# A threshold search that sets two bits per step from three counts, on one Trainium2 core

## Chip, core and metric

The kernel runs on one core of a Trainium2 chip. The metric is the device time in microseconds (us) of one execution, as the median of several. The engines are named as the profile names them: PE is TensorE (PEld its weight loads), DVE is VectorE, ACT is ScalarE, POOL is GpSimd, SP is SyncE, which issues most DMAs. SBUF and PSUM are the on-chip memories; only PE's results go to PSUM first.

## What is computed

One inference step of a decoder of two layers for two groups of rows: a prompt of 512 rows and a sample group of 8 sequences with 4 new rows each, which has a cache of 2048 keys per sequence. In each layer, half of the channels go through a gated mix over chunks, the other half through sparse attention: a light indexer scores all keys, and each query attends to the best k of them only. Then come an output projection, layer norms, a feed-forward block and a gated embedding. The part that matters here is the selection for the sample group (k = 256 of 2052):

```python
def sample_sparse_attn(q, k_new, v_new, qi, wi, ki_new, ck, cv, cki, page_table):
    ...
    I = indexer_scores(qi, wi, ki_all)
    tpos = PAST_LEN + jnp.arange(T)
    causal = jnp.arange(L)[None, :] <= tpos[:, None]
    I = jnp.where(causal[None], I, -jnp.inf)
    _, idx = lax.top_k(I, TOPK_SAMPLE)
    ...
    return attend_selected(q, k_sel, v_sel, valid)
```

## The kernel before

All 544 rows stay on the chip. A product of 32-bit matrices is made from three products of split operands (a rounded part `hi` or `h`, and the rest `lo` or `l`), so most of PE's work is in triples of matmuls with 272 or 256 columns. The weights come from memory in chunks (`raw`), ACT rounds them (`hi`), DVE or POOL subtracts (`lo`).

The order of all instructions is fixed when the kernel is built. The work is written as some fifty generators (`backbone`, `s_scores`, `unit` and so on); each says before a piece of work which engine it takes and for how long, and `Sched.run` lays the pieces out one after the other by estimated start times and by a table of priorities (`PR`, weights `WP` and `WO`). At run time each engine then takes its instructions in that order, and semaphores hold it where data isn't there.

`s_scores` works once per layer. It makes the scores of the sample queries (`y.I`, 128 partitions with 513 scores each: a query's keys are spread over four partitions) and finds for each query the threshold that just 256 scores exceed, as a bit pattern of a 32-bit number from the highest bit down:

- `count(thr)` (lines 1300 to 1307) has ACT take the sign of (threshold - score) over the 513 scores and add the signs up in `cf` (line 1302; the signs themselves go to the scratch `maskb`). PE multiplies `cf`, 128 x 1 and 32 bits wide, by the constant matrix `gallf`, which adds up the four partitions of a query (the matmul's own line is that of the helper `mm`, 828).
- DVE compares the sum with a limit and makes the bit (line 1315), and sets it in `c` together with the next bit to try (line 1317).
- One count with the threshold zero (`zero`) decides on the sign (lines 1310 and 1311), then 31 steps follow, one bit each.

So 32 counts a layer go round ACT, PE and DVE. A 16-bit copy of the same matrix, `gall`, serves three products after the search. Around the search, other generators fill the engines: on DVE above all the top-k of the prompt's queries (`MAX8` and `MATCH_REPLACE8`, lines 1229 and 1231) and the rotations (`rope`, lines 1006 to 1012); on PE the backbone's products (`mm<-hi,Ah` and its kin), the rotated sample queries spread over partitions (`at<-cp,u` in `q_sample`), the transposes of gathered keys (`at<-ident,w`, line 1689 in `s_qk`) and their small products with the sample queries (`at<-w,QB` in `s_kt`); on ACT and DVE the evictions from PSUM (`copy`, lines 865 and 867) and the gated mix (lines 1490 to 1553).

Of the kernel before, what the change touches and what calls it, by code (L numbers as in the profile page):

```python
# [8 lines left out]
F32 = mybir.dt.float32  # L9
F32R = mybir.dt.float32r  # L10
BF16 = mybir.dt.bfloat16
F16 = mybir.dt.float16
# [44 lines left out]
WO = 10.415  # L57
PR = {'q_sample': 10.5, 'free_raw': 7.5, 'gmix': 2.0, 'evac_c1': 11.0, 's_scores': 17.0, 's_block': 14.0, 'mix_b': 3.5, 'load_r': 8.5, 'kidx': 14.5, 's_attn': 3.0, 'evac_au': -2.5, 'head': 1.5, 's_kt': 6.0, 'loads': 3.0, 'evac_q': -4.0, 'sgu_load': 14.0, 's_relu': 1.5, 'mix_a': 14.5, 'setup1': 6.0, 's_attn_f': 12.5, 'gmlp': 4.5, 'unit': 0.0, 'load_pe': 6.5, 'evac_oa': 1.0, 'backbone': -6.5, 'evac_c0': -1.5, 'setup2': 0.5, 'splits': -2.5, 's_qk': 6.0, 'gnorm': 1.0, 'store': 7.0, 'setup': 6.0, 'wout22': -0.5, 'wadd': 12.0, 'mtee': 4.0, 'fin': 0.5, 'wsum': 7.0, 'wcopy': 0.5, 'evac_p': 10.0, 'ln1': 5.0, 'moving': -1.0, 'vload': 15.5, 'split_x': 12.0, 'evac_f2': 16.5, 'warm': 8.0, 'wsplit': 5.0, 'mv': 5.0, 'evac_o': 9.5, 'wout': 11.5, 'ln2': 10.5, 'evac_g': 3.0}
# [354 lines left out]
def build(tc, I, O, cols):  # L413
# [15 lines left out]
    def const(name, shape, dt=F32):  # L429
        return sb.tile(list(shape), dt, tag=name, name=name)  # L430
# [18 lines left out]
    gallf = const("gallf", [128, 128])  # L449
# [89 lines left out]
    def setup2():  # L539
# [6 lines left out]
        G.tensor_copy(gallf, st[:, 0:128])  # L546
# [700 lines left out]
    def s_scores(y):  # L1247
# [43 lines left out]
        cf = sm("cf", [128, 1])  # L1291
        c = sm("c", [128, 1], I32)
        d = sm("d", [128, 1], I32)
# [3 lines left out]
        dp = ps[:, 8:9].bitcast(I32)  # L1297
        lim = NQ - 2 * STOP + 0.5

        def count(thr):  # L1300
            yield [("A", 707.0)]
            A.activation(y.maskb, Iv, AF.Sign, scale=-1.0, bias=thr, accum_out=cf)
            S.cur.ready += MARGIN
            yield [("P", 140.0)]
            mm(ps[:, 0:1], gallf, cf, True, True)
            S.cur.ready += 100.0
# [3 lines left out]
        V.tensor_scalar(d, ps[:, 0:1], lim, -float(2 ** 31), op0=ALU.is_gt, op1=ALU.mult)  # L1310
        V.tensor_scalar(c, d, 31, 2 ** 30, op0=ALU.arith_shift_right, op1=ALU.bitwise_xor)
        for bit in range(30, -1, -1):
            yield from count(c.bitcast(F32))
            yield [("V", 70.0)]
            V.tensor_scalar(dp, ps[:, 0:1], lim, float(2 ** bit), op0=ALU.is_gt, op1=ALU.mult)
# [1125 lines left out]
```

## Time and profile before

| | us |
|---|---|
| median of 3 runs | 1504.61 (1498.2 to 1511.35) |
| profiled execution | 1507.94 |
| its span, first to last instruction | 1506.1 |
| PE busy | 1452.1 (96%) |
| DVE busy | 1094.3 (73%) |
| ACT busy | 800.5 (53%) |
| POOL busy | 159.9 (11%) |

The profile is of one execution. Its durations are in us or ns; the start of a row is counted from the start of the span. Matmuls overlap in the pipeline, so the time that one costs is read from end to end (start plus duration), not from its duration. Idle time in front of an instruction is shown in brackets with what ended it.

### The profile page before, as it was taken

The page shows a single profiled execution, that of the slowest core. Times are in us where ns is not written, and L with a number is a line of the kernel's source. Part 1 is how long each engine was busy: PE and PEld are TensorE (multiplying, and loading weights), DVE is VectorE, ACT ScalarE, POOL GpSimd, SP SyncE. Part 2 cuts the span into 40 slices and gives each one's busy share as a digit, 9 for nine tenths or more (in the row PEclk, how much of TensorE's full clock was granted, in tenths as well). Part 3 has the DMA queues.
Part 4 walks back from the last instruction along what each step waited for, and adds up shares of the span by engine and source line. Part 5 has one row for each costly group of instructions (what it writes and reads, how often), then busy time and mean ns, then how long its engine had stood idle before and what let it go on. Part 6 is the DMA issues. An engine that isn't in the chain of part 4 may idle for free.

```text
span 1506.1 us, 31220 instructions
## 1 busy us (share of the span) xinstructions
PE 1452.1 (96%) x12262; PEld 1381.6 (92%) x12262; DVE 1094.3 (73%) x2867; ACT 800.5 (53%) x1865; POOL 159.9 (11%) x192
## 2 busy tenths in 40 slices
PE   9998999999999999999999889999999999999997
PEld 8787888799999999999987788788999999999996
DVE  5699886588965948567666998856979567484765
ACT  6747766464642715335376478663737345172443
POOL 2123421120000000001001234110200000000000
PEclk9999899999999999999999999999999999999998
DMA  7644431422231322315044425332122313232211
GB/s 236 201 147 125 146 128 59 142 85 71 85 127 57 126 86 74 123 58 185 34 149 146 155 90 175 112 135 82 69 85 99 126 57 113 76 107 99 82 60 60
DMA packets 55474, 164.47 MB, mean 109 GB/s; under 512 B 7648, under 2 KB 15008, under 8 KB 55328
## 3 DMA queue, kind: packets, MB, share of 16 engines
q1 hardware_dynamic: 44960, 124.73, 25.0%
q0 software_dynamic: 10368, 37.75, 7.6%
q8 instruction: 96, 1.57, 0.4%
q14 instruction: 50, 0.41, 0.1%
HBM read 156.09 MB, written 6.37 MB: 108 GB/s over the span
## 4 chain that ended last, share of the span: by engine, by line
PE 82%; DVE 11%; ACT 3%; DMA 2%; issue 2%; another core or an unknown queue 1%; SPq 0%; ACTq 0%; DVEq 0%
PE at L828 41%; PE mm L828 37%; DVE u L1231 2%; DVE m L1229 2%; PE at L1689 1%; PE at L1597 1%; DVE ga L861 1%; DMA raw<-in_w_c 1%; DVE t L1530 1%; DMA raw<-in_w_au 0%; PE at L1857 0%; DMA Bh<-in_x 0%; DMA w<-in_ck,idxK 0%; DVE u L1553 0%
## 5 line engine op out<-in xcount | busy, mean ns | idle before, releaser
L731 ACT CAST hi<-raw 128x1024 fp32r<-128x1024 f32 (+5 forms) x137 | 139.1, 1020 | 188.8 <-PE mm L828 89.9
L828 PE MATMUL mm<-Bh,hi 128*128 128x272 f32 x584 | 171.5, 294 | 1.3 <-DVE t L1010 0.8
L828 PE MATMUL mm<-Ah,hi 128*128 128x272 f32 x584 | 170.8, 293 | 0.3
L735 DVE TENSOR_TENSOR lo<-raw,hi 128x1024 fp32r<-128x1024 f32 (+5 forms) x122 | 144.5, 1184 | 34.8 <-ACT hi L731 34.0
L828 PE MATMUL mm<-Bl,hi 128*128 128x272 f32 x584 | 169.3, 290 | 0.0
L828 PE MATMUL mm<-Bh,lo 128*128 128x272 f32 x584 | 168.8, 289 | 0.0
L828 PE MATMUL mm<-Al,hi 128*128 128x272 f32 x584 | 168.7, 289 | 0.0
L828 PE MATMUL mm<-Ah,lo 128*128 128x272 f32 x584 | 168.2, 288 | 0.0
L828 PE MATMUL at<-w,hi 128*128 128x272 f32 x704 | 159.3, 289 | 0.0
L2069 DVE TENSOR_TENSOR u<-u,mm 128x272 f32<-128x272 f32 x96 | 42.0, 437 | 120.0 <-PE mm L828 119.0
L690 ACT CAST hi<-u 128x512 fp32r<-128x512 f32 x128 | 73.1, 619 | 96.9 <-PE mm L828 40.7
L828 PE MATMUL at<-w,lo 128*128 128x272 f32 x416 | 120.0, 288 | 0.0
L828 PEld LDWEIGHTS at<-w,hi 128*128 128x128 f32 x704 | 119.6, 188 | 0.0
L828 PEld LDWEIGHTS mm<-Bh,hi 128*128 128x128 f32 x584 | 110.7, 189 | 2.7 <-ACT hi L731 1.3
L690 ACT CAST hi<-raw 128x1024 fp32r<-128x1024 f32 x64 | 53.4, 834 | 112.4 <-PE at L828 43.7
L828 PEld LDWEIGHTS mm<-Ah,hi 128*128 128x128 f32 x584 | 110.0, 188 | 1.6 <-DVE u L1905 0.7
L828 PEld LDWEIGHTS mm<-Bh,lo 128*128 128x128 f32 x584 | 110.8, 190 | 0.3
L828 PEld LDWEIGHTS mm<-Bl,hi 128*128 128x128 f32 x584 | 110.5, 189 | 0.0
L828 PEld LDWEIGHTS mm<-Ah,lo 128*128 128x128 f32 x584 | 110.1, 189 | 0.2
L828 PEld LDWEIGHTS mm<-Al,hi 128*128 128x128 f32 x584 | 109.8, 188 | 0.0
L828 PE MATMUL at<-Bl,hi 128*128 128x272 f32 x376 | 108.6, 289 | 0.0
L828 PE MATMUL at<-Ah,lo 128*128 128x272 f32 x376 | 108.6, 289 | 0.0
(389 smaller groups left out, 4405.8 us busy)
## 6 DMA issues: line engine op xcount, KB each, us to landing
raw<-in_w_f SPq DMA_DIRECT2D x128, 512.0 KB
raw<-in_w_q SPq DMA_DIRECT2D x16, 512.0 KB
raw<-in_w_o SPq DMA_DIRECT2D x16, 512.0 KB
raw<-in_w_g SPq DMA_DIRECT2D x16, 512.0 KB
raw<-in_w_au SPq DMA_DIRECT2D x8, 512.0 KB
raw<-in_w_av SPq DMA_DIRECT2D x8, 512.0 KB
u<-in_x SPq DMA_DIRECT2D x8, 272.0 KB
hD<-t SPq DMA_DIRECT2D x16, 136.0 KB
```

What stands on the lines that cost most here:

```text
L690: A.copy(hi[:, :n], x)
L731: A.copy(c.hi[:, a:b], c.raw[:, a:b])
L735: E.tensor_tensor(c.lo[:, a:b], c.raw[:, a:b], c.hi[:, a:b].bitcast(F32), op=ALU.subtract)
L828: PE.matmul(out, l, r, start=start, stop=stop, skip_group_check=True)
L861: f(*args, **kw)
L1229: V.max(m8, work[:, :N])
L1231: V.match_replace(work[:, :N], m8, work[:, :N], -3.3e38)
L1530: E.tensor_tensor(av[:n, :256], av[:n, :256], y.sb[:n, hs], op=ALU.add)
L1597: PE.transpose(p[:, c * 128:(c + 1) * 128], P[:, c * 128:(c + 1) * 128], ident)
L1689: PE.transpose(p[:, t, :], raw[:, (g * 4 + t) * 128:(g * 4 + t + 1) * 128], ident)
L2069: V.tensor_tensor(r[:, a:b], r[:, a:b], ps[:, :n], op=ALU.add)
```

## The change

A step now sets two bits. Three thresholds are tried at once (the two bits as 01, 10 and 11), ACT makes three sign passes into three columns of `cf`, and one product counts for all three; the number of counts above the limit (0 to 3) is the pair of bits. `cf` is half precision now, which holds sums of 513 signs exactly, and the matrix is `gall`; `gallf` is gone. 15 steps set 30 bits, a count before them decides on the sign and one behind them on the last bit. DVE has three operations behind each count (compare and add up; scale to a bit pattern; set it in three thresholds) and a fourth that prepares the next step's pattern (`pre`) while ACT counts. The patterns come from a table (`tab`), which DVE writes into the counts' PSUM tile before the first count. The table of priorities and its weight `WO` have changed, too (13 entries of `PR`).

```diff
-WO = 10.415
+WO = 10.199
...
-        G.tensor_copy(gallf, st[:, 0:128])
...
-        cf = sm("cf", [128, 1])
-        c = sm("c", [128, 1], I32)
-        d = sm("d", [128, 1], I32)
+        cf = sm("cf", [128, 3], F16)
+        c = sm("c", [128, 3], I32)
...
         ps = yield Al("at", [128, 512])
-        dp = ps[:, 8:9].bitcast(I32)
+        di = ps[:, 8:9].bitcast(I32)
+        pre = sm("pre", [128, 3], I32)
+        tab = ps[:, 16:64].bitcast(I32).rearrange("p (k j) -> p k j", j=3)
+        yield [("V", 70.0 * 19)]
+        for j in range(3):
+            V.memset(tab[:, 0, j:j + 1], (j + 1) * 2 ** 29)
+        for i in range(1, 15):
+            V.tensor_scalar(tab[:, i, :], tab[:, i - 1, :], 0.25, None, op0=ALU.mult)
+        V.memset(tab[:, 15, :], 1)
+        V.tensor_copy(pre, tab[:, 0, :])
         lim = NQ - 2 * STOP + 0.5
 
-        def count(thr):
-            yield [("A", 707.0)]
-            A.activation(y.maskb, Iv, AF.Sign, scale=-1.0, bias=thr, accum_out=cf)
+        def count(*thr):
+            for j, t in enumerate(thr):
+                yield [("A", 707.0)]
+                with nc.allow_low_precision(reason="sums of 513 signs are exact"):
+                    A.activation(y.maskb, Iv, AF.Sign, scale=-1.0, bias=t, accum_out=cf[:, j:j + 1])
             S.cur.ready += MARGIN
             yield [("P", 140.0)]
-            mm(ps[:, 0:1], gallf, cf, True, True)
+            mm(ps[:, :len(thr)], gall, cf[:, :len(thr)], True, True)
             S.cur.ready += 100.0
 
         yield from count(zero)
         yield [("V", 270.0)]
-        V.tensor_scalar(d, ps[:, 0:1], lim, -float(2 ** 31), op0=ALU.is_gt, op1=ALU.mult)
-        V.tensor_scalar(c, d, 31, 2 ** 30, op0=ALU.arith_shift_right, op1=ALU.bitwise_xor)
-        for bit in range(30, -1, -1):
-            yield from count(c.bitcast(F32))
+        V.tensor_scalar(di, ps[:, 0:1], lim, -float(2 ** 31), op0=ALU.is_gt, op1=ALU.mult)
+        V.scalar_tensor_tensor(c, di.to_broadcast([128, 3]), 31, pre, op0=ALU.arith_shift_right, op1=ALU.bitwise_xor)
+        for i in range(15):
+            k = 29 - 2 * i
             yield [("V", 70.0)]
-            V.tensor_scalar(dp, ps[:, 0:1], lim, float(2 ** bit), op0=ALU.is_gt, op1=ALU.mult)
+            V.scalar_tensor_tensor(pre, tab[:, i + 1, :], 2 << k, c[:, 0:1].to_broadcast([128, 3]), op0=ALU.bitwise_xor, op1=ALU.bitwise_xor)
+            yield from count(*(c[:, j:j + 1].bitcast(F32) for j in range(3)))
             yield [("V", 70.0)]
-            V.scalar_tensor_tensor(c, dp, (2 ** (bit - 1)) if bit else 0, c, op0=ALU.bitwise_xor, op1=ALU.bitwise_xor)
+            V.tensor_scalar(ps[:, 4:7], ps[:, 0:3], lim, None, op0=ALU.is_gt, op1=ALU.add, accum_out=c2)
+            yield [("V", 70.0)]
+            V.tensor_scalar(di, c2, float(2 ** k), None, op0=ALU.mult)
+            yield [("V", 70.0)]
+            V.tensor_tensor(c, di.to_broadcast([128, 3]), pre, op=ALU.bitwise_xor)
+        c = c[:, 0:1]
+        yield from count(c.bitcast(F32))
+        yield [("V", 140.0)]
+        V.tensor_scalar(di, ps[:, 0:1], lim, None, op0=ALU.is_gt)
+        V.tensor_tensor(c, di, c, op=ALU.bitwise_xor)
         thr = c.bitcast(F32)
```

How the instructions stand now, at three places. Lines below 1285 are two lower in the changed kernel than in the one before, and a number behind a name only tells buffers apart.

DVE at the start of the first layer's search, before: `u_838` are the scores, `u_1478` and `u_1480` the rotation of the sample queries, `u_982` and `u_761` the prompt's top-k.

```order
L1287 TENSOR_SCALAR u_838<-at_847 128x512
L861 TENSOR_TENSOR ga_1438<-gs_935 128x4
L1231 MATCH_REPLACE u_982<-m_1273,u_982 128x256
L861 SCALAR_TENSOR_TENSOR gq_937<-gq_937,ga_1438 128x4
L1231 MATCH_REPLACE u_761<-m_1173,u_761 128x512
L1006 TENSOR_TENSOR u_1478<-at_574,cp 128x512
L861 TENSOR_SCALAR gq_937<-gq_937 128x4
L1009 TENSOR_TENSOR u_1480<-at_574,cp 128x8x32
L1010 TENSOR_TENSOR u_1480<-at_574,cp 128x8x32
L861 TENSOR_SCALAR gy_1439<-gq_937 128x4
L1012 TENSOR_TENSOR u_1478<-u_1478,u_1480 128x512
L1310 TENSOR_SCALAR d<-at_1461 128x1
```

And in the changed kernel, where `u_1451` and `u_1453` are the rotation and `at_1460` the tile of the counts with the table:

```order
L1285 TENSOR_SCALAR u_836<-at_845 128x512
L1004 TENSOR_TENSOR u_1451<-at_572,cp 128x512
L1299 MEMSET at_1460 128x1 x3
L1301 TENSOR_SCALAR at_1460<-at_1460 128x3 x14
L1302 MEMSET at_1460 128x3
L1303 COPY pre<-at_1460 128x3
L1007 TENSOR_TENSOR u_1453<-at_572,cp 128x8x32
L1008 TENSOR_TENSOR u_1453<-at_572,cp 128x8x32
L859 TENSOR_TENSOR ga_1436<-gs_933 128x4
L1010 TENSOR_TENSOR u_1451<-u_1451,u_1453 128x512
L859 SCALAR_TENSOR_TENSOR gq_935<-gq_935,ga_1436 128x4
L1229 MATCH_REPLACE u_980<-m_1271,u_980 128x256
```

The table's 19 operations stand inside the rotation, and the replacements of the top-k, which stood ahead of the rotation, stand behind it.

PE between two counts in the first half of the first layer's search, before (`at_1461` are the counts):

```order
L828 MATMUL at_1461<-cf,gallf 128x1
L1689 MATMUL at_2070<-ident,w_1639 128x128 x4
L1689 MATMUL at_2081<-ident,w_1639 128x128 x4
L828 MATMUL at_2090<-w_1919,QB 32x128 x4
L828 MATMUL at_2091<-w_1919,QB 32x128 x4
L828 MATMUL at_2090<-w_2069,QB 32x128 x4
L828 MATMUL at_2091<-w_2069,QB 32x128 x4
L828 MATMUL at_1461<-cf,gallf 128x1
```

And in the changed kernel, between the seventh and the eighth count of three (`at_1460`):

```order
L826 MATMUL at_1460<-cf,gall 128x3
L826 MATMUL at_1940<-w_1947,QB 32x128 x4
L826 MATMUL at_1941<-w_1947,QB 32x128 x4
L1707 MATMUL at_1998<-ident,w_1705 128x128 x4
L1707 MATMUL at_2024<-ident,w_1705 128x128 x4
L826 MATMUL at_1940<-w_1997,QB 32x128 x4
L826 MATMUL at_1941<-w_1997,QB 32x128 x4
L1707 MATMUL at_2039<-ident,w_1927 128x128 x4
L1707 MATMUL at_2060<-ident,w_1927 128x128 x4
L826 LDWEIGHTS gall
L826 MATMUL at_1460<-cf,gall 128x3
```

Two groups of small products stand between the counts in both, with eight transposes before and sixteen now.

ACT around one count early in the first layer's search, before (`t_` are tiles of the gated mix):

```order
L867 COPY w_1547<-at_1548 128x512
L1302 ACTIVATE maskb,cf<-u_838,c 128x513
L1490 ACTIVATE t_1560,gs_941<-at_1576 32x128
L1525 ACTIVATE t_1378<-t_1378,gn_1440,gy_1439 128x128
L1490 ACTIVATE t_1560,gs_941<-at_1576 32x128
```

And in the changed kernel, the second step's three passes:

```order
L729 CAST hi_1464<-raw_1452 128x1024
L1310 ACTIVATE maskb,cf<-u_836,c 128x513
L865 COPY w_1567<-at_1599 128x512
L1310 ACTIVATE maskb,cf<-u_836,c 128x513
L1508 ACTIVATE t_1563,gs_939<-at_1577 32x128
L1310 ACTIVATE maskb,cf<-u_836,c 128x513
```

Three passes stand where one stood, with a copy and an activation of other work between them.

## Rows read from the trace of the kernel before

**Rows 1.** From the page: busy time of each engine, and the chain by engine.

```profile
PE 1452.1 (96%) x12262; PEld 1381.6 (92%) x12262; DVE 1094.3 (73%) x2867; ACT 800.5 (53%) x1865; POOL 159.9 (11%) x192
...
PE 82%; DVE 11%; ACT 3%; DMA 2%; issue 2%; another core or an unknown queue 1%; SPq 0%; ACTq 0%; DVEq 0%
```

**Rows 2.** Stretches: length; busy us of PE, PEld, DVE, ACT, POOL; clock, DMA share, GB/s.

```profile
100.00:212.00 112.00, 100.19 (x946) 90.10 (x939) 102.19 (x366) 80.26 (x222) 38.52 (x42) 0.92 0.41 131
849.00:958.00 109.00, 96.65 (x940) 86.73 (x933) 98.61 (x364) 81.97 (x228) 41.28 (x44) 0.95 0.44 144
```

**Rows 3.** Timeline of PE around one count: start us, duration us, engine and operation.

```profile
139.34 0.28 PE L828 MATMUL mm<-lo,Ah 128*128 128x256 f32 x1
139.45 0.28 PE L828 MATMUL at<-cf,gallf 128*128 128x1 f32 x2
139.59 0.36 PE L828 MATMUL mm<-hi,Ah 128*128 128x256 f32 x1
139.79 0.27 PE L828 MATMUL mm<-hi,Al 128*128 128x256 f32 x1
```

**Rows 4.** Timeline of PE around a half-precision count behind the search.

```profile
211.64 0.29 PE L828 MATMUL mm<-Al,hi 128*128 128x272 f32 x1
211.77 0.18 PE L828 MATMUL at<-cnt,gall 128*128 128x1 f16 x1
211.81 0.37 PE L828 MATMUL mm<-Ah,hi 128*128 128x272 f32 x1
```

**Rows 5.** Waits of PE by releaser: us in total, times, longest us.

```profile
PE at L828 <- ACT maskb L1302: 6.7, 7, 1.8
...
PE at L828 <- DVE d L1310: 1.6, 1, 1.6
```

**Rows 6.** Timeline of all engines in one quick step of the second search.

```profile
881.02 0.28 PE L828 MATMUL at<-cf,gallf 128*128 128x1 f32 x2
...
881.33 0.17 DVE L1315 TENSOR_SCALAR at<-at 128x1 int32<-128x1 f32 x1
...
881.60 0.16 DVE L1317 SCALAR_TENSOR_TENSOR c<-at,c 128x1 int32<-128x1 int32 x1
...
881.86 0.73 ACT L1302 ACTIVATE maskb<-u,c 128x513 bf16<-128x513 f32 x1
...
882.49 0.19 ACT L1302 ACTIVATION_READ_ACCUMULATOR maskb<-u,c 128x1 f32 x1
```

**Rows 7.** Timeline of PE in the first search: small products and transposes.

```profile
134.29 1.08 PE L828 MATMUL at<-w,QB 128*32 128x128 f32 x32
135.30 1.09 PE L1689 MATMUL at<-ident,w 128*128 128x128 f32 x8
136.15 0.36 PE L828 MATMUL mm<-hi,Ah 128*128 128x256 f32 x1
```

**Rows 8.** Timeline of DVE at the start of the first search.

```profile
101.37 0.68 DVE L1287 TENSOR_SCALAR u<-at 128x512 f32<-128x512 f32 x1
...
103.16 0.68 DVE L1006 TENSOR_TENSOR u<-at,cp 128x512 f32<-128x512 f32 x1
...
105.22 0.15 DVE L1310 TENSOR_SCALAR d<-at 128x1 int32<-128x1 f32 x1
105.41 0.15 DVE L1311 TENSOR_SCALAR c<-d 128x1 int32<-128x1 int32 x1
105.48 0.15 DVE L861 TENSOR_TENSOR ga<-gy 128x4 f32<-128x4 f32 x1
```

**Rows 9.** As rows 2: the pieces of the searches in which the PE clock was lowered.

```profile
100.00:115.00 15.00, 13.05 (x109) 8.85 (x102) 14.84 (x57) 7.77 (x27) 3.31 (x2) 0.77 0.58 200
...
145.00:160.00 15.00, 11.88 (x99) 10.06 (x98) 12.62 (x49) 9.53 (x23) 4.08 (x6) 0.68 0.38 118
...
849.00:865.00 16.00, 12.25 (x99) 8.68 (x92) 15.08 (x58) 9.85 (x31) 3.30 (x2) 0.79 0.57 198
...
895.00:910.00 15.00, 13.65 (x135) 12.60 (x134) 13.69 (x54) 9.44 (x26) 7.21 (x12) 0.89 0.09 25
```

More of the change, by code (lines that the diff above doesn't have):

```diff
@@ L56 @@
 WP = 0.698
-WO = 10.415
-PR = {'q_sample': 10.5, 'free_raw': 7.5, 'gmix': 2.0, 'evac_c1': 11.0, 's_scores': 17.0, 's_block': 14.0, 'mix_b': 3.5, 'load_r': 8.5, 'kidx': 14.5, 's_attn': 3.0, 'evac_au': -2.5, 'head': 1.5, 's_kt': 6.0, 'loads': 3.0, 'evac_q': -4.0, 'sgu_load': 14.0, 's_relu': 1.5, 'mix_a': 14.5, 'setup1': 6.0, 's_attn_f': 12.5, 'gmlp': 4.5, 'unit': 0.0, 'load_pe': 6.5, 'evac_oa': 1.0, 'backbone': -6.5, 'evac_c0': -1.5, 'setup2': 0.5, 'splits': -2.5, 's_qk': 6.0, 'gnorm': 1.0, 'store': 7.0, 'setup': 6.0, 'wout22': -0.5, 'wadd': 12.0, 'mtee': 4.0, 'fin': 0.5, 'wsum': 7.0, 'wcopy': 0.5, 'evac_p': 10.0, 'ln1': 5.0, 'moving': -1.0, 'vload': 15.5, 'split_x': 12.0, 'evac_f2': 16.5, 'warm': 8.0, 'wsplit': 5.0, 'mv': 5.0, 'evac_o': 9.5, 'wout': 11.5, 'ln2': 10.5, 'evac_g': 3.0}
+WO = 10.199
+PR = {'q_sample': 10.5, 'free_raw': 7.5, 'gmix': 2.5, 'evac_c1': 11.0, 's_scores': 17.0, 's_block': 10.0, 'mix_b': 3.5, 'load_r': 9.5, 'kidx': 12.5, 's_attn': -1.5, 'evac_au': -3.5, 'head': 1.5, 's_kt': 6.0, 'loads': 3.0, 'evac_q': -4.0, 'sgu_load': 15.0, 's_relu': 1.5, 'mix_a': 14.5, 'setup1': 6.0, 's_attn_f': 12.5, 'gmlp': 4.5, 'unit': -1.0, 'load_pe': 6.5, 'evac_oa': 1.0, 'backbone': -6.5, 'evac_c0': -1.5, 'setup2': 0.5, 'splits': -2.5, 's_qk': 6.0, 'gnorm': 1.0, 'store': 7.0, 'setup': 6.0, 'wout22': -0.5, 'wadd': 12.0, 'mtee': 4.0, 'fin': -1.0, 'wsum': -0.5, 'wcopy': 9.0, 'evac_p': 10.0, 'ln1': 5.0, 'moving': -1.0, 'vload': 15.5, 'split_x': 8.0, 'evac_f2': 16.5, 'warm': 5.5, 'wsplit': 5.0, 'mv': 5.0, 'evac_o': 9.5, 'wout': 11.5, 'ln2': 10.5, 'evac_g': 3.0}
 TBS = (3, 1, 2, 0)
@@ L448, in build @@
     gall = const("gall", [128, 128], F16)
-    gallf = const("gallf", [128, 128])
     gneg = const("gneg", [128, 128], F16)
```

## Prediction

> **What bounds the kernel now.** I read the page's busy times and chain first: TensorE (PE) is busy for 96% of the span, and the chain that ended last runs on PE for 82% [rows 1]. So a microsecond comes off the end only if it comes off PE's stream. The next view is the table of stretches. The threshold search of the sample group runs once per layer, in the stretches from 100 to 212 us and from 849 to 958 us; in these 112 and 109 us PE is busy for 100.2 and 96.7 us only and VectorE (DVE) is busy for 102.2 and 98.6, ScalarE (ACT) for 80.3 and 82.0 [rows 2]. What is lost there is 24 us of waiting, plus what a lower clock costs. The search is a serial loop, ACT counts signs, PE sums over partitions, DVE sets a bit, and PE takes its instructions in a fixed order, so a count that isn't ready stops everything behind it. The changed order differs from the old one on PE only inside these two stretches and the 35 to 45 us behind each (two runs of some 930 and 950 rows of 10,215); before, between and after them it is the same row for row.
>
> **The counts on PE.** Now each of the 64 counts (32 a layer) is a product with 32-bit operands and takes two passes, x2 in its row [rows 3]. In a dense place the product before the count ends at 139.34 + 0.28 = 139.62 us and the one behind it at 139.59 + 0.36 = 139.95, where the next follows after 0.11 to 0.12: the count costs 0.33 - 0.12 = 0.21 us [rows 3]. The trace has a count with half-precision operands too, made after the search: 211.64 + 0.29 = 211.93 to 211.81 + 0.37 = 212.18, which is 0.25 - 0.12 = 0.13 us [rows 4]. Its width of one column should hold for three. Afterwards there are 17 counts a layer: 64 x 0.21 = 13.4 us become 34 x 0.13 = 4.4 us, **-9.0 us**, all on the path. The bounds are 0.06 (the count hidden under the load for the next) and 0.21, that is -11.4 and -6.3.
>
> **The waits for counts.** PE waits 6.7 us in 7 places for the sign pass [rows 5]. These places go with their steps, **-6.7 us**, and new ones come. How long is a step when nothing is in its way? In one of the quickest the count starts at 881.02, DVE's two operations at 881.33 and 881.60, the sign pass at 881.86, and its sum is read by 882.49 + 0.19 = 882.68 [rows 6]; with 0.2 for the way back to PE, an estimate (DVE started 0.03 after the count's end), that is 1.9 us. The new step has two more sign passes at 0.82 each (0.63 to the sum's read and 0.19 for it; all three write the same scratch, so each waits for the one before), one more DVE operation at 0.27 and a second sum to read: 1.9 + 1.64 + 0.27 + 0.2 = 4.0 us. What does the order give PE to do meanwhile? 32 records of small products (two groups) take 135.30 - 134.29 = 1.0 us and eight transposes 136.15 - 135.30 = 0.9 [rows 7]. At the place shown in the order, early in the search, PE has two groups of small products and sixteen transposes between two counts, 1.0 + 1.8 = 2.8 us against 4.0: 1.2 us of waiting. The second step has the same and one product of 256 columns, 0.4 more: 0.8 of waiting. The others hold 4 to 6 us by the same costing, about 4.7 on the mean, and I put no wait on them. For two layers: 2 x (1.2 + 0.8) = **+4.0 us**. The bounds are 0 (PE behind its plan anyhow) and 0.5 for each of 30 steps, 15 us.
>
> The Trainium skill ("ScalarE: Activation LUTs", section "What ACT_TABLE_LOAD costs") has an activation with a pointer for its bias at about 280 ns + 0.833 ns an element, and back-to-back ones overlapping by 93 ns: by the page three passes over 513 would be an estimated 1.94 us. The rows have 0.82 for one with the read of its sum, which the page doesn't count, so the rows' 2.5 us stands; by the page the new waits would be some 2.4 us smaller.
>
> **The table.** Before the loop DVE now builds a table of 3 x 16 words in PSUM, 19 small operations in one block, each waiting for the one before. Two dependent ones start 105.22 and 105.41, 0.19 apart; an independent one follows at 105.48, 0.07 later [rows 8]. So the block takes 17 x 0.19 + 2 x 0.07 = 3.4 us, with bounds of 1.3 and 3.6. The order puts it into the rotation of the sample queries, behind that rotation's first product, while two replacements of the prompt's top-k that stood ahead go behind it. These filled 102.05 (101.37 + 0.68) to 103.16, 1.1 us [rows 8]. So the rotation, done shortly before 105.3 now, ends 3.4 - 1.1 = 2.2 to 2.3 us later; I take 2.2. PE has nothing else in its order there: it stands idle for 1.6 us at this very place, set down to DVE's operation of line 1310 [rows 5]. That grows to 3.8: 2 x 2.2 = **+4.4 us**, with bounds of 0 and 2 x 3.6. Next the first count of three: on DVE the two replacements and two operations, until about 109.0, then three sign passes, count ready at about 111.7; PE's work behind the rotation (2.0 us at full clock, twice that at half) is through at 109.5 to 111.5. I take the middle, 1.3 us, so **+2.6 us** for two layers.
>
> **The rest.** The 15 extra counts a layer put 30 x 0.82 = 25 us onto ACT, which has 30 us free in each stretch [rows 2]. The copy of the 32-bit matrix on GpSimd goes, early and long before use: nothing. The new priorities move some rotations from GpSimd to DVE, evictions between ACT and DVE, and on SP one weight load by five places: nothing on the mean, but they are why the range is wide: -8 to +8, as large as the waits for DVE and evictions in these stretches. The later feed-forward stretches have the same PE order and hardly a wait.
>
> **Sum.** -9.0 - 6.7 + 4.0 + 4.4 + 2.6 = -4.7 us. The profiled execution took 1507.94, so 1503.2 on its footing; the median of the runs is 1504.61, 3.3 lower and inside 1498.2 to 1511.35. I forecast 1504.6 - 4.7 = 1500 us, with 1491 to 1508 for this case by itself.
>
> **Rivals.** First, the clock stays up. The granted clock was 0.77, 0.68, 0.79 and 0.89 in four pieces of the search [rows 9]; from full speed and half speed (2.4 and 1.2 GHz) that is 6.9 + 9.6 + 6.7 + 3.3 = 26.5 us at half, costing 13 us. The pieces lie where PE waits, for counts among others. If half as many steps leave fewer holes, up to 13 us come on top: 1487, or 1493 if only the two later pieces go. Against it: the start, where two of the pieces lie, gets more idle, not less. The Trainium skill ("TensorE: Matmul & The Clock Gate", "What's actually happening") says that the low clock is the resting state which activity lifts; by that rule the longer wait for the table keeps the start at half speed, and the trace agrees that the start is low (0.77).
>
> Second, DVE is the bound of the stretch. It is over 90% busy [rows 2], and it gets the table (3.4) and, for 64 operations of 0.16, some 64 again with 15 reads of sums, put at half an operation: 3.4 + 15 x 0.08 = 4.6 us more a layer. Where PE only follows DVE, its saving becomes waiting: 1504.6 + 9.2 = 1514. Against it: few of PE's waits are DVE's, and the prompt's top-k, most of DVE's load, is work whose place can move.
>
> Third, the three passes on ACT take over: slower. The order now puts other work between the three passes of a step (a copy, an activation at the place shown). At a sign pass's 0.82 each, two such make the step 5.6 us, and with DVE's queue ahead of its four operations 6.0. Against 4.7 us of PE work that is 1.3 x 30 = 39 us of waits, less 9.0 and 6.7, so 1504.6 + 23 = 1528. It decides from a mean step of 5.2 us. Against it: these orders were laid out with such work in the count.
>
> **How the numbers follow.** Forecast 0.46, clock 0.30, DVE 0.16, ACT 0.08. A median of this kernel tells about 1% from no change, 1489.6 and 1519.7. Faster: most of the clock's case and the lower edge of mine, 0.28. Slower: nearly all of ACT's case and the upper edge of DVE's, 0.08. Same: 0.64. The range of 1484 to 1515 holds the first three cases nearly whole.
>
> **What would show it.** Right: 34 count records in half precision, each 0.13 us between its neighbours; PE waiting near 4 us for the rotation at both starts; about 1 us of waiting at the count behind the sixteen transposes; steps of 4.5 to 6 us and a search some 10 to 15 us shorter. Wrong: a table much shorter than 3 us, waits for the sign pass above 15 us in all, or a granted clock of 1.00 in the pieces named. A time under 1489 would mean that the waits and the clock, not the counts, were what the search cost.

## The result, and the profile after

The changed kernel takes 1521.82 us in the median of 4 runs (1518.59 to 1522.28), against 1505.4 for the kernel before beside it: a ratio of 1.0117, with an interval of 1.0087 to 1.0147. It is slower, by 1.2% where 0.3% faster was forecast. Two later groups of runs, on other occasions, gave 1.0144 (1.0100 to 1.0188) and 1.0053 (1.0032 to 1.0075). The changed kernel's median was 1522 to 1526 in all three; that of the kernel before was 1502 to 1505 twice and 1512 to 1515 in the other groups, at much the same granted clocks (0.974 to 0.982 in the one kind, 0.971 to 0.982 in the other). So the sign holds, and the size lies between 0.5 and 1.4%. Why the level of the kernel before moves by 10 us from one group to the next was not found; groups 2 and 3 of the table below, one of either kind, ran on the same chip.

The page of the changed kernel, in answer to [rows 1]: busy times and the chain by engine.

```profile
PE 1454.3 (96%) x12168; PEld 1381.6 (91%) x12168; DVE 1115.6 (73%) x2961; ACT 813.3 (53%) x1898; POOL 147.5 (10%) x176
...
PE 76%; DVE 16%; ACT 3%; DMA 3%; issue 2%; SPq 0%; POOL 0%; ACTq 0%; DVEq 0%
```

DVE is busy for 21 us more, and its share of the chain went from 11 to 16%, while PE's fell by 6 points. Next the stretches of [rows 2], and the whole stage from the eviction of the scores to the first tanh behind the attention, layer by layer (columns: stretch, its length, busy us of PE, PEld, DVE, ACT, POOL, clock). First the changed kernel:

```profile
100.00:212.00 112.00, 93.23 (x913) 81.54 (x912) 107.17 (x409) 87.60 (x250) 34.81 (x35) 0.92 0.44 145
849.00:958.00 109.00, 91.38 (x891) 79.60 (x890) 103.54 (x394) 87.52 (x255) 36.78 (x40) 0.92 0.46 144
...
103.12:346.87 243.75, 219.82 (x2075) 197.81 (x2068) 198.92 (x707) 159.80 (x422) 54.30 (x50) 0.92 0.34 115
855.44:1097.48 242.04, 217.95 (x2071) 195.66 (x2064) 197.16 (x698) 161.03 (x426) 52.97 (x54) 0.94 0.35 116
```

The same two stages in the kernel before:

```profile
102.05:339.44 237.39, 219.66 (x2122) 198.24 (x2115) 189.80 (x660) 151.24 (x395) 63.23 (x61) 0.96 0.36 118
848.97:1082.72 233.75, 217.00 (x2130) 195.81 (x2123) 186.68 (x657) 154.38 (x402) 57.58 (x58) 0.97 0.36 120
```

This table holds the result. The stages are 6.4 and 8.3 us longer, 14.7 us together, and the span grew by 14.5; the rest of the program is as long as before. PE's free time in them (length less busy) goes from 17.7 and 16.8 to 23.9 and 24.1 us, **13.5 us more**. PE's busy time is the same to 1.1 us, though its counts should take 9 us less: the clock is 0.92 and 0.94 in place of 0.96 and 0.97, which I read as slower matmuls using up what the counts gave. DVE is busy 9.1 and 10.5 us longer. In the first search, 100 to 212 us, it is now busy for 107.2 of 112 us, 96%.

The searches themselves did come out shorter: from the first count to the last 96.6 and 89.8 us, where the kernel before has 106.6 and 103.1. The stages are longer all the same, for other work of PE moved behind the searches (in the first layer it is busy for 136.9 us there, 123.9 before). Of PE's 13.5 us of new waiting 10.1 lie in front of the last counts, and the clock fell most behind the last counts, from there to the end of the stage: from 0.99 to 0.92 in the first layer (209.6 to 339.4 us before, 203.9 to 346.9 now) and from 0.99 to 0.95 in the second.

The counts themselves cost what was forecast. The timeline of PE around a count of three:

```profile
160.28 0.28 PE L826 MATMUL mm<-lo,Ah 128*128 128x256 f32 x1
160.40 0.18 PE L826 MATMUL at<-cf,gall 128*128 128x3 f16 x1
160.44 0.37 PE L826 MATMUL mm<-hi,Ah 128*128 128x256 f32 x1
```

From 160.56 to 160.81 are 0.25 us, less 0.12 for the product behind: 0.13, as with one column in [rows 4]. The waits of PE, in answer to [rows 5] (us in total, times, longest):

```profile
PE at L826 <- DVE gy L859: 7.6, 2, 4.6
PE at L826 <- ACT maskb L1310: 6.2, 4, 2.2
PE at L826 <- DVE pre L1303: 4.8, 2, 2.4
PE at L826 <- DVE t L1357: 4.2, 2, 3.6
...
PE at L826 <- DVE gq L859: 2.6, 2, 1.3
```

The wait for the sign pass is where it was (6.2 us for 6.7); four waits for DVE, 19.2 us in all, are new or longer: three for small operations, and `t`, the 513-wide comparison behind the search. One is the table. DVE's and PE's timelines at the start of the first search (in brackets PE's idle time in front):

```profile
103.73 0.33 DVE L1299 MEMSET at<- 128x1 int32 x3
104.09 2.82 DVE L1301 TENSOR_SCALAR at<-at 128x3 int32<-128x3 int32 x14
106.99 0.06 DVE L1302 MEMSET at<- 128x3 int32 x1
107.09 0.16 DVE L1303 COPY pre<-at 128x3 int32<-128x3 int32 x1
...
107.30 0.16 PE L826 MATMUL at<-cf,gall 128*128 128x1 f16 x1 [2.40 <-DVE pre L1303]
```

The table takes 3.5 us (107.25 less 103.73). PE waits 2.4 us for it and 1.3 for the rotation (`gq`) behind it. Another wait is a stall beside POOL, the longest of PE's row for `gy`:

```profile
147.70 2.98 DVE L859 SCALAR_TENSOR_TENSOR gy<-ga,gy 128x4 f32<-128x4 f32 x1
148.29 2.36 POOL L733 TENSOR_TENSOR lo<-raw,hi 128x1024 fp32r<-128x1024 f32 x1
...
152.16 0.66 PE L826 MATMUL at<-w,QB 128*32 128x128 f32 x8 [4.59 <-DVE gy L859]
```

An operation of four columns, 0.15 us elsewhere, ends as POOL's subtraction ends (150.68 and 150.65), and PE stands still for 4.6 us, the stall and what DVE still had to do behind it. The Trainium skill ("SBUF — State Buffer", section "SBUF: two separate sides") has a DVE operation with two SBUF inputs and a GpSimd operation that reads SBUF lock each other out: the one that starts first has the port for its whole length. These rows agree in that the two end together. They do not bear out the order: DVE's row starts 0.59 us before POOL's, and DVE is the one held up. The kernel before has such stalls, too, the longest of 3.02 us at 865.7.

### The profile page after: what moved, and what is told of

It is laid out like the page before. It is cut to its first block, busy times and chain, and to the rows that moved or that the text cites. A ratio compares the mean times of both kernels' runs of the same rounds, so it can differ in the third digit from the quotient of the medians.

```text
span 1520.6 us, 31091 instructions
## 1 busy us (share of the span) xinstructions
PE 1454.3 (96%) x12168; PEld 1381.6 (91%) x12168; DVE 1115.6 (73%) x2961; ACT 813.3 (53%) x1898; POOL 147.5 (10%) x176
## 4 chain that ended last, share of the span: by engine, by line
PE 76%; DVE 16%; ACT 3%; DMA 3%; issue 2%; SPq 0%; POOL 0%; ACTq 0%; DVEq 0%
PE at L826 38%; PE mm L826 35%; DVE u L1229 3%; DVE m L1227 3%; DMA w<-in_cv,idxV 1%; PE at L1615 1%; DVE lo L733 1%; DVE ga L859 1%; ACT maskb L1310 1%; DVE w L863 1%; DMA raw<-in_w_c 1%; DMA Bh<-in_x 0%; PE at L1875 0%; DVE u L1601 0%; PE at L1707 0%
## 5 line engine op out<-in xcount | busy, mean ns | idle before, releaser
L733 DVE TENSOR_TENSOR lo<-raw,hi 128x1024 fp32r<-128x1024 f32 (+3 forms) x123 | 147.1, 1196 | 39.6 <-ACT hi L729 39.5
L826 PE MATMUL mm<-Ah,hi 128*128 128x272 f32 x584 | 174.5, 299 | 0.6 <-DVE u L1913 0.3
L826 PE MATMUL at<-Al,hi 128*128 128x272 f32 x376 | 108.9, 290 | 0.0
```

The lines of the kernel that those rows point to most:

```text
L733: E.tensor_tensor(c.lo[:, a:b], c.raw[:, a:b], c.hi[:, a:b].bitcast(F32), op=ALU.subtract)
L826: PE.matmul(out, l, r, start=start, stop=stop, skip_group_check=True)
```

## The experiments

Eighteen runs were made, in five groups, each group on one chip beside the kernel before. Ratios are to that kernel in the same group, with their 95% intervals. The expectations speak of theories. A: the steps of the new search are too long for the order. B: the new order places the work badly. C: DVE's small operations stall beside POOL's subtractions. D: what the change puts on DVE costs. E: the extra sign passes on ACT cost.

| group | before, us | run | us | ratio |
|---|---|---|---|---|
| 1 | 1512.5 | f16_onebit | 1511.3 | 0.9980 (0.9962 to 0.9999) |
| 1 | | table_ready | 1522.5 | 1.0063 (1.0042 to 1.0084) |
| 1 | | one_pass | 1520.7 | 1.0054 (1.0035 to 1.0072) |
| 1 | | new_search_old_numbers | 1527.1 | 1.0085 (1.0065 to 1.0106) |
| 2 | 1502.5 | after_again | 1526.2 | 1.0144 (1.0100 to 1.0188) |
| 2 | | table_ready_one_pass | 1517.2 | 1.0098 (1.0074 to 1.0123) |
| 2 | | subtract_on_dve | 1517.5 | 1.0096 (1.0061 to 1.0130) |
| 2 | | table_ready_replanned | 1525.5 | 1.0138 (1.0095 to 1.0181) |
| 3 | 1515.0 | two_bits_old_order | 1522.5 | 1.0057 (1.0040 to 1.0075) |
| 3 | | two_bits_old_order_table | 1525.2 | 1.0060 (1.0043 to 1.0077) |
| 3 | | after_less_topk | 1512.4 | 0.9989 (0.9974 to 1.0003) |
| 3 | | before_less_topk | 1498.6 | 0.9891 (0.9873 to 0.9909) |
| 4 | 1514.5 | after_third | 1521.7 | 1.0053 (1.0032 to 1.0075) |
| 4 | | before_more_dve | 1525.0 | 1.0082 (1.0056 to 1.0108) |
| 4 | | after_copies_on_act | 1525.3 | 1.0074 (1.0050 to 1.0098) |
| 4 | | f16_copies_on_act | 1512.0 | 0.9991 (0.9971 to 1.0010) |
| 5 | 1513.8 | two_bits_old_order_two_passes | 1525.1 | 1.0073 (1.0054 to 1.0091) |
| 5 | | f16_more_act | 1516.0 | 1.0020 (1.0006 to 1.0035) |

### One part of the change, or one part undone

**f16_onebit** does one part alone, in the kernel before:

```diff
-        cf = sm("cf", [128, 1])
+        cf = sm("cf", [128, 1], F16)
...
-            mm(ps[:, 0:1], gallf, cf, True, True)
+            mm(ps[:, 0:1], gall, cf, True, True)
```

> The kernel before with one thing changed: the sums of the signs and the matrix that adds them are half precision, so each of the 64 counts is one pass on PE and not two. The order on PE, DVE and ACT is that of before. By the rows of before a count goes from 0.21 to 0.13 us: 64 x 0.08 = 5 us less work on PE. If PE's work bounds the search (the reasoning of the prediction), the time falls by those 5 us, to 1500. If the search is bound by the chain of the steps and what feeds PE, the saving turns into waiting and the time stays at 1504 to 1506. The granted clock shows no change by either.

Measured: 0.998, some 3 us by the ratio for the 5 us taken from PE (0.2 to 5.7 by its interval; the medians lie 1.2 us apart). It is the lowest ratio of a kernel that does all the work.

**table_ready** makes the table in the program's setup, on POOL; **one_pass** makes one sign pass a step and leaves two out, so that it no longer finds the threshold; **table_ready_one_pass** does both.

```diff
+        for j in range(3):
+            G.memset(tab[:, 0, j:j + 1], (j + 1) * 2 ** 29)
+        for i in range(1, 15):
+            G.tensor_scalar(tab[:, i, :], tab[:, i - 1, :], 0.25, None, op0=ALU.mult)
...
-        for j in range(3):
-            V.memset(tab[:, 0, j:j + 1], (j + 1) * 2 ** 29)
...
+                  if j == 0:
```

> The changed kernel with the table of 3 x 16 words made once at the program's start by GpSimd, in SBUF, so that 18 of the 19 operations at the start of each search are gone from DVE; the order on PE and ACT is the same row for row. Theory A (the steps of the new search are too long for the order: table, three passes, four operations): PE's 3.7 us of waiting at the start of each search fall to 1 or less and the steps behind start 2 to 3 us earlier, 4 to 7 us in all: 1515 to 1518. Theory B (the new numbers place the work badly, the search itself is not what costs): the 3 us show up again at the next wait, 1520 to 1522. Theory C (DVE's small operations stall beside GpSimd's subtractions): the time changes by less than 3 us either way, by which operation happens to meet a subtraction.

> The changed kernel with one sign pass a step in place of three; the other two counts of a step are sums of zeros, so the search is left out in its meaning and its bits are not those of the reference, while all of its products and DVE's operations stay; the order on PE and DVE is the same row for row, but for one memset a layer. It takes 2 x 0.82 us from each of 30 steps, 49 us of ACT's work on the chain of the search. Theory A (steps too long): the waits of PE in the search go from 18 and 15 us to about 10 each, as before the change, and the clock returns: 1506 to 1512. Theory B (numbers) and theory C (stalls beside GpSimd): ACT was no bound, the time stays above 1517.

> The changed kernel with both cuts: the table made at the program's start, and one sign pass a step in place of three (the bits of the search are not the reference's). The order on PE is the same. Apart the two cuts took 0.5 and 0.6% off the ratio of 1.012. Theory A (the steps and the table are too long for the order): both add up, 1.001 or less, that is 16 us under the changed kernel, and with 9 us less of PE's work the ratio can go to 0.995. Theory C (what is left is DVE stalled beside GpSimd, or the order's own): 1.003 to 1.007, no more than either cut alone.

Measured: 1.0063 and 1.0054, no less than the 1.0053 that the changed kernel itself has beside a kernel before of the same level (after_third). Both cuts together gave 9 us on the changed kernel of their own group (1.0098 for 1.0144), with intervals that overlap, and still stand 1% above the kernel before. So the table and the passes are a part of the loss at most, and theory A falls as the main cause: one_pass takes 41 us off ACT (771.9 for 813.3 us busy on the pages) and gains nothing clear. For the table the answer is clouded by a price of its own: its 18 small operations on POOL delayed the first gather of the indexer's keys, and PE waited for that before the search began. The wait is in all five profiles with the table on POOL and in none with it on DVE; table_ready, waits of PE in the first 110 us:

```profile
PE at L1063 <- DMA w<-in_cki,idxI: 2.8, 1, 2.8
```

**after_again** and **after_third** are the changed kernel as it is:

> The changed kernel once more as it is, for its profile and its ratio on the chip of the three runs beside it. Every theory: a ratio of 1.009 to 1.015 to the kernel before, and per layer 24 us of waiting of PE between the scores and the first tanh.

> The changed kernel as it is, beside the three others on one chip. Every theory: 1.009 to 1.016 to the kernel before.

The second missed its range: 1.0053, with 1521.7 us as ever, beside a kernel before at 1514.5.

**subtract_on_dve** takes POOL's 1024-wide subtractions during the searches to DVE:

```diff
+                if S.search and b - a == 1024:
+                    E = V
```

> The changed kernel with the 1024-wide subtractions of the weights' low parts that GpSimd makes during the searches (7 in all, 2.36 us each) made by DVE, in the same place of the order; PE, ACT and SP have the same rows. It takes away what DVE's small operations stall beside (stalls of 2 to 2.8 us, 7 of them in the searches) and gives DVE 7 times some 1.1 us of its own work. Theory C (the stalls are what costs): PE's waits for gy and t, 7.6 and 4.2 us, fall to under 3 in all and the ratio comes to 1.003 to 1.007. Theory A: DVE has only more to do in a search that its steps bound; the ratio stays at 1.010 to 1.016.

Measured: 1.0096, 8.7 us under the changed kernel of its group, again with intervals that overlap. PE's waits for `gy` and `t` went from 7.3 + 4.3 to 2.7 + 3.7 us, but it now waits 9.6 us in 7 places for the subtractions on DVE. The stalls beside POOL are a part of the loss at most.

### The order

**new_search_old_numbers** has the search of the change with `WO` and `PR` of before; **table_ready_replanned** plans anew for a ready table, with the rotations' small operations kept off POOL's subtractions in the plan.

> The changed kernel's search with the scheduler's numbers (weight and priorities) of the kernel before. Theory B (the new numbers place the work badly): the time comes to the prediction's sum or below, 1495 to 1503. Theory A (steps too long for any order whose costs are the planner's): 1515 to 1530, with PE waiting over 15 us in each search. Theory C: the stalls beside GpSimd fall elsewhere, 1510 to 1525.

> The changed kernel with the table made at the program's start and the planner told so (70 ns in place of 1330 for the start), and with the small operations of the rotations marked for the planner as ones that do not run beside a GpSimd subtraction. The order is planned anew from there. Theory A and C together: each search starts 3.5 us earlier and PE does not wait for gy beside a subtraction, ratio 0.995 to 1.003. Theory B (it is the placing that costs, and any new plan throws dice): anywhere from 0.995 to 1.015, with waits at new places.

Measured: 1.0085 and 1.0138. Other orders of the new search are no better, and the first lies where theory A had it (1515 to 1530), not B (1495 to 1503). The strongest test of the order is **two_bits_old_order**, where the new step fills the slots of two old ones and PE's order is that of before, 30 counts fewer:

```diff
+            yield from slots(lambda: (sign(0, t[0]), sign(1, t[1])), lambda: None)
...
+            yield from slots(lambda: sign(2, t[2]), lambda: total(3))
```

> The new search laid into the order of the kernel before: planner's costs, numbers and slots are those of before, and a step of two bits fills the slots of two old steps (two sign passes in the first, the third and the product in the second), with the table made at the program's start by GpSimd. PE's order is that of before but for 30 counts fewer; so the search is as long as before and its steps have twice the time. Theory B (the new order packs the search too tightly: the form itself costs little): the counts' 9 us are gained and some of the 6.7 of waits: ratio 0.990 to 0.997, 1490 to 1500. Theory D (DVE's extra operations a step cost wherever they lie) or A (the three passes cost wherever they lie): ratio 1.003 to 1.012.

> As the run beside it (the new search in the order of before), but with the table made by DVE in PSUM at the start of each search, as in the changed kernel; no time is planned for it. Every theory: PE waits some 2 to 4 us more at the start of each search, 4 to 8 us in all on the run beside it, if nothing takes them up again.

> two_bits_old_order with one of the three sign passes of each step left out (the third count is a sum of zeros, so the bits are not the reference's): ACT makes 32 passes a layer as the kernel before does, while the counts on PE and the operations on DVE are those of the new search and PE's order is that of before. Theory E (the 30 extra passes, 28 us on ACT, are what eats the saving): from 1.006 to 0.993 to 0.998, the half and more of the 9.5 us that PE saves. If it is DVE's longer chain a step, or PE's saving is hidden in any case, it stays at 1.003 to 1.007.

Measured: 1.0057, with the table on DVE 1.0060 (no slower by its ratio, where 4 to 8 us more of waiting were expected), and with a pass less a step 1.0073. Theory B falls: the new search is slower in the old order too. So does theory E for this order: without the extra passes it is not faster. No run took back that a step's chain on DVE is longer. What the waits do is the lesson of these runs. PE's longest waits in the first layer's stage (100 to 340 us), first in f16_onebit, which has 32 counts there:

```profile
PE at L826 <- ACT maskb L1301: 3.9, 5, 2.0
PE at L826 <- DVE gs L859: 3.9, 1, 3.9
PE at L826 <- DVE t L1529: 3.8, 2, 1.9
PE at L826 <- ACT u L865: 2.2, 1, 2.2
```

and in two_bits_old_order_two_passes, which has 17 in steps of twice the length:

```profile
PE at L832 <- DVE t L1556: 5.4, 4, 2.3
PE at L832 <- ACT w L871: 4.9, 3, 3.0
PE at L832 <- issue: 2.6, 4, 1.1
PE at L832 <- ACT u L871: 2.4, 1, 2.4
```

The waits for the sign pass are as good as gone (0.8 us of 3.9), and waits for DVE's `t` and ACT's evictions have taken their place. This group of runs is not explained in full: all three are 12 to 14 us above f16_onebit by their ratios. The late start by POOL's table may be 2 to 4 us of it in the two that have one (the scores' eviction ends at 104.2 and 106.1 us in place of 101.8; the runs without that table have 100.7 to 103.3); the rest stays open.

### DVE's load

**after_less_topk** and **before_less_topk** leave out every other replacement of the prompt's top-k during the searches; **before_more_dve** makes every other MAX8 twice.

```diff
-                V.match_replace(work[:, :N], m8, work[:, :N], -3.3e38)
+                if not (S.search and S.alt % 2):
+                    V.match_replace(work[:, :N], m8, work[:, :N], -3.3e38)
...
+                if S.search and S.alt % 2:
+                    V.max(m8, work[:, :N])
```

> The changed kernel with every other replacement of the prompt's top-k left out while a search runs (some 16 a layer at 0.61 us with its load, 10 us a layer of DVE's work; the prompt's masks are then not the reference's). PE, ACT, GpSimd and SP have the same rows. Theory D (in the new order DVE bounds the search, and PE, its clock included, waits for it): the time falls by 14 us or more, ratio 1.003 or less. Theory A (the chain of the steps bounds it) or B: it falls by less than 6 us, ratio 1.008 or more.

> The kernel before with the same replacements left out during its searches, as its pair. If DVE bounds the search of before as well, it falls by as much as the changed kernel does, 10 us or more, ratio under 0.994; if PE and the chain of single steps bound it, by less than 5 us, ratio 0.997 or more. What the changed kernel loses more than it here is what DVE's load costs in the new order.

> The kernel before with nothing of the change, but with every other MAX8 of the prompt's top-k made twice while a search runs (31 in all, 17 us of DVE's work, near the 21 us that DVE's busy time grew by with the change). PE, ACT, GpSimd and SP have the same rows, the output is the same. Theory D (DVE bounds the searches, and what it gets, PE loses, in idle time and in clock): 10 to 20 us slower, ratio 1.007 to 1.014, which is the changed kernel's loss. If DVE has slack that takes it up, or PE and the chain of the steps bound the search: less than 5 us, ratio under 1.003.

Measured: 0.9989, 0.9891 and 1.0082. The pages' busy times, of after_less_topk, then before_less_topk, then before_more_dve, last after_third:

```profile
PE 1442.7 (96%) x12168; PEld 1370.6 (91%) x12168; DVE 1096.8 (73%) x2899; ACT 813.0 (54%) x1898; POOL 150.3 (10%) x176
```

```profile
PE 1449.5 (97%) x12262; PEld 1382.8 (92%) x12262; DVE 1081.0 (72%) x2805; ACT 801.3 (53%) x1865; POOL 166.0 (11%) x192
```

```profile
PE 1460.9 (96%) x12262; PEld 1389.5 (91%) x12262; DVE 1108.2 (73%) x2896; ACT 800.6 (53%) x1865; POOL 161.2 (11%) x192
```

```profile
PE 1452.2 (96%) x12168; PEld 1379.4 (91%) x12168; DVE 1110.4 (73%) x2961; ACT 813.5 (54%) x1898; POOL 149.6 (10%) x176
```

Read DVE's column beside the medians of groups 3 and 4, whose kernel before is at 1514.5 to 1515.0. The old search goes 1498.6, 1515, 1525.0 us with DVE at 1081.0, 1094.3 [rows 1], 1108.2; the new one 1512.4 and 1521.7 us at 1096.8 and 1110.4. PE has the same rows within each kind. **So work put on DVE costs time in the old search, and work taken off gains time in both, with PE's rows as they were:** roughly 0.7 to 1.2 us for each us of the column (the 1094.3 is of the first occasion's page). 16 us of useless MAX8 (29 of 548 ns) on the kernel before, 14 in the column, cost 0.8%, the order of the change's own loss. So far theory D stands.

That the change is slower because of its load on DVE is not shown. The line through the old search's upper points (10.0 us for 13.9, 0.72 for each) speaks for it: at the new search's loads it has 1516.8 and 1526.6 us, 4 to 5 more than the new search takes. Three things speak against it. The column counts a stall beside POOL as busy time, and three pages of the changed kernel have 1115.6, 1116.0 (after_again) and 1110.4, a spread worth 4 us on that line. With less top-k in both, the two kernels stand 1.0% apart (0.9989 and 0.9891), no less than the 0.5% with all of it (after_third), though a loss that came from a full DVE should have shrunk. And in the old order the new search has hardly more load on DVE than the kernel before and is still slower; the pages of two_bits_old_order and two_bits_old_order_two_passes:

```profile
PE 1452.6 (96%) x12168; PEld 1378.3 (91%) x12168; DVE 1096.4 (72%) x2899; ACT 822.1 (54%) x1925; POOL 166.4 (11%) x209
```

```profile
PE 1454.8 (96%) x12168; PEld 1381.3 (91%) x12168; DVE 1097.3 (72%) x2901; ACT 803.8 (53%) x1865; POOL 164.6 (11%) x209
```

The line has 1516.5 and 1517.2 us for them, and 1522.5 and 1525.1 were measured. The next two runs show another limit of theory D.

**after_copies_on_act** and **f16_copies_on_act** move DVE's load to ACT with nothing left out:

```diff
+        if v and S.search and n == 512:
+            S.alt += 1
+            v = S.alt % 2
```

> The changed kernel with half of the 512-wide evictions that the planner gave to DVE during the searches made by ACT, in the same place of the order (19 copies of 0.69 us go from DVE, ACT gets them at 0.58); the output is the same, PE has the same rows. Theory D: 13 us less on DVE, 6 to 13 us less time, ratio 1.002 to 1.008. Theory A (the chain with its three passes on ACT bounds the search): ACT's 11 us more make the steps longer, no gain or a loss, ratio 1.012 or more.

> The version that should beat both by theory D: the search of before, one bit a step, with half-precision sums (ratio 0.998 by itself) and half of the 512-wide evictions that the planner gave to DVE during the searches made by ACT (16 copies, 11 us off DVE, 9 us onto ACT, which is at 73 to 76% there). Theory D: 6 to 10 us less on top, ratio 0.991 to 0.994. Otherwise 0.997 to 1.001.

Measured: 1.0074 and 0.9991, no gain on 1.0053 and 0.998. By the pages 7.0 and 9.4 us went from DVE and 8.3 and 7.0 onto ACT (against f16_onebit in the second). What was taken off DVE helped when it vanished, not when ACT had to do it. One reading is that an eviction on ACT stands in a queue with the sign passes: PE waits for ACT's `w` 5.3 us in 6 places in after_copies_on_act, against 2.4 us in 4 places in the changed kernel. **f16_more_act** prices the passes themselves:

```diff
+                if twice:
+                    A.activation(y.maskb, Iv, AF.Sign, scale=-1.0, bias=thr, accum_out=cx)
```

> f16_onebit (one bit a step, half-precision sums, ratio 0.998) with 15 more sign passes a layer, one behind every second step's own, into a column that nothing reads: 27 us more on ACT, as the three-count step has, without making any step's own chain longer. The output is the same, PE and DVE have the same rows. Theory E (ACT's load in the search is paid for in time): 6 to 15 us slower, ratio 1.002 to 1.008. If ACT's free time takes them up, as the prediction had it: 0.997 to 1.000.

Measured: 1.0020 against 0.998 in another group, some 6 us (2 to 10 by the intervals) for 22 us of ACT by the pages (822.3 for 800.4), though no step's own sum waits for these passes. The prediction had them at nothing. So theory E holds in the old search; but taking passes out of the new one gained nothing in either order (one_pass, two_bits_old_order_two_passes), so how much of the change's loss is theirs stays open.

## Why the prediction was wrong

**The counts: right as work, wrong as time.** Half precision and 30 counts fewer are 0.13 us a count as forecast. The sum took PE's work at one for one; in f16_onebit 5 us of it gave some 3, with an interval from nearly nothing to all of it. The steps came out at 6.0 and 5.6 us on the mean and the searches 10 and 13 us shorter, both named as signs of being right, and the time rose.

**"A microsecond comes off the end only if it comes off PE's stream": the step that failed.** The chain and PE's 96% told of the whole program. In the searches DVE stood at 91% [rows 2]. With PE's rows as they were, 16.4 us came off the old search when DVE had less top-k (1498.6 for 1515.0) and 10.5 went on when it had more; work on ACT cost some 6. What was put on DVE or ACT in these stretches was paid in time, and the sum had the change's work there at nothing but for the waits that it foresaw. The share of each engine's waits misled: a wait of PE is put to what ended it, and an operation of DVE that came late because DVE was full reads like any other.

**The waits gone, -6.7: wrong.** They did not go with the counts. In the changed kernel the wait for the sign pass is still 6.2 us, and where the steps had time to spare (two_bits_old_order_two_passes) other waits came in their place. The +4.0 set against them was near for the sign passes (6.2 measured), but by luck: the waits came at the third and sixth step of each search, and none at the two places forecast. The place shown in the order lies between the sixth and the seventh count of three (144.95 and 154.93 us), not the seventh and eighth; PE reached the count behind its sixteen transposes late, after the stall of 4.6 us, and did not wait there for a sign pass. (The 2.4 us in the paragraph behind it should have been 2.1: four waits, 2.46 less 1.94 each.)

**The table, +4.4: right.** 3.5 us of DVE for 3.4, and PE waits 2.4 + 1.3 = 3.7 us for 3.8 at both starts. That the first count would wait for it too, by the tile that both use, was not seen. The wait for the first count of three, +2.6, did not come: PE reached it at 113.4 and 865.7 us without idling.

**The rest, at nothing: wrong, twice.** The 25 us on ACT were not free: 22 cost some 6 in the old search (f16_more_act). The new placing put work on DVE: rotations went from POOL to DVE (of their last additions POOL had 12 and has 6), and in the two stages DVE is busy for 19.6 us more. The bounds of -8 to +8 were for this and were too narrow for PE's 13.5 us of new waiting.

**The rivals.** The second, DVE as the bound, comes closest to what the runs show, with a load close to the truth: 4.6 us a layer in the stretches of [rows 2], where 5.0 and 4.9 came (107.17 less 102.19, 103.54 less 98.61). It had 0.16. Its 1514 was low; it counted the two stretches alone, 9.2 us, where the whole stages have 19.6, and left out the clock. The third had the length of a step (6.0 and 5.6 us on the mean against its limit of 5.2, by the counts' starts) but not what follows: the waits for the sign pass stayed at 6.2 us where it had 39. The first went the other way. In answer to [rows 9], the changed kernel:

```profile
100.00:115.00 15.00, 9.90 (x94) 6.26 (x93) 14.09 (x61) 7.24 (x27) 0.00 (x0) 0.77 0.37 140
145.00:160.00 15.00, 9.62 (x82) 8.66 (x82) 14.24 (x54) 10.46 (x24) 5.18 (x4) 0.77 0.49 149
849.00:865.00 16.00, 11.47 (x98) 8.76 (x100) 15.12 (x64) 6.82 (x33) 0.00 (x0) 0.87 0.52 191
895.00:910.00 15.00, 10.02 (x95) 8.46 (x93) 14.62 (x65) 11.17 (x26) 5.18 (x4) 0.77 0.64 203
```

The pieces stayed low, two somewhat higher and one lower, and a new one came behind the search, where the kernel before had 1.00 from 216 to 246 us:

```profile
216.00:246.00 30.00, 28.09 (x198) 23.83 (x197) 17.38 (x59) 14.71 (x35) 0.77 (x1) 0.72 0.05 19
```

PE waited 1.6 us for DVE's `mx` at 216.8, and its dense products then ran at a lowered clock. That the clock fell because of the waits was not tried by itself; no run filled the waits with other products.

**What stays open:** the 10 us by which the kernel before moves between groups, what the new search costs in the old order beyond the late start, and how the change's loss is shared among DVE's load, the passes on ACT, the longer chain of a step and the clock.

## What to carry to other kernels

Look for the engine that is full in the stretch, not in the whole program, and price a change on every engine it loads: here 5 us off PE gave some 3, and work on DVE or ACT cost time with PE's stream unchanged. To find what a stretch is sensitive to, add useless work to one engine at a time in an unchanged order, and take some away: two runs tell what the list of waits does not. Where several engines of a stretch are nearly full (PE, DVE and ACT at 83, 96 and 78% from 100 to 212 us), moving work between them may gain nothing; two kernels here gained nothing by it, while leaving work out gained in two. And put the explanation to the same test as the prediction: a run with the load of before and the time of the change shows that the load is not all of it.

## What was not expected of the hardware

A DVE operation that also gives out its sum costs a second instruction of 0.14 us on DVE (30 of them, 4.2 us), as on ACT (0.19); 15 steps with four operations and a read took 23.3 us of DVE in both layers, more than the 19.5 of 31 steps with two. And the same kernel in the same order differs by 10 us between groups of runs at an equal granted clock, so that only ratios within a group, or groups whose kernel before stands level, can be compared.

The rows behind the first of these, DVE's groups in the changed kernel, then in the kernel before:

```profile
L1328 DVE TENSOR_SCALAR at<-c 128x1 int32<-128x1 f32 x30 | 4.8, 162 | 1.0
L1323 DVE SCALAR_TENSOR_TENSOR pre<-at,c 128x3 int32<-128x3 int32 x30 | 4.8, 161 | 1.0
L1330 DVE TENSOR_TENSOR c<-at,pre 128x3 int32<-128x3 int32 x30 | 4.8, 160 | 2.2
...
L1326 DVE TENSOR_SCALAR_CACHE_REDUCE at<-at 128x3 f32<-128x3 f32 x30 | 4.7, 157 | 0.4 <-PE at L826 0.4
L1326 DVE DVE_READ_ACCUMULATOR at<-at 128x1 f32 x30 | 4.2, 140 | 0.0
```

```profile
L1317 DVE SCALAR_TENSOR_TENSOR c<-at,c 128x1 int32<-128x1 int32 x62 | 9.8, 158 | 5.6 <-DVE at L1315 0.5
L1315 DVE TENSOR_SCALAR at<-at 128x1 int32<-128x1 f32 x62 | 9.7, 157 | 6.7 <-PE at L828 5.0 <-PE at L1597 1.4 <-issue 0.2
```
